# First mixer of a two-layer trunk: the value and gate block as one float32 product, and some copies and scalings on ScalarE

## The chip, the core and the metric
The kernel runs on one core of a Trainium2 chip. The metric is the device time of one execution in microseconds (us); lower is better. The engines are TensorE (PE; its weight loads PEld), VectorE (DVE), ScalarE (ACT), GpSimd (POOL) and SyncE (SP), which issues the transfers. Each engine takes its own instructions in order and waits on semaphores of the others.

## The reference, cut to what matters
Input x is 256 tokens of 1024 numbers. Two layers follow, each a mixer and a mixture of experts with layer norms. The change lies in the first layer's mixer:

```python
proj = x @ w_in
qa, kc, vc, ksl, vsl, kw, vw, ga, qm, km, vm = jnp.split(proj, EVEN_SPLITS, axis=-1)
qa = rope(heads(qa, NSA_HEADS), positions)       # kc, ksl, kw likewise
gates = jax.nn.sigmoid(ga.astype(jnp.float32)).astype(x.dtype).reshape(B, S, NSA_HEADS, 3)
o_a = nsa_attention(qa, kc, heads(vc, NSA_KV_HEADS), ksl, heads(vsl, NSA_KV_HEADS),
                    kw, heads(vw, NSA_KV_HEADS), gates, ...)
o_b = moba_attention(rope(heads(qm, MOBA_HEADS), positions),
                     rope(heads(km, MOBA_HEADS), positions), heads(vm, MOBA_HEADS))
return jnp.concatenate([o_a, o_b], axis=-1) @ w_out
```
Inside nsa_attention, keys and values (kc, vc) are compressed: overlapping blocks of 32 tokens, a position term, a two-layer network with gelu, and softmax scores of the queries against the 15 compressed blocks. With 256 tokens the selected-block branch and the window branch both reduce to causal softmax attention over all tokens.

## The kernel before, in words
Tokens lie in two tiles of 128 (t = 0, 1; NT = 2), the 1024 inputs in eight chunks of 128 (NCH = 8). The projection runs in six blocks of columns: w0[0] (kc, ksl, kw, vc; 512 columns), w0g (vsl, vw, gates; 280), w0[1] (queries of A; 512), then w0[2] to w0[4] (queries, keys, values of B). "First", "second" and "third block" below are the first three of these.

For accuracy a block is split: ACT rounds the weights to fp32r (wh, L190, in `split`), DVE subtracts to get the remainder (wl, L193), x has been split likewise (xh, xl), and `proj_nat` adds three products per chunk and token tile on PE (L244 xh·wh, L245 xl·wh, L246 xh·wl): 48 products a block. wh and wl of two chunks share a buffer of three. The accumulators `acc` are four banks. The unsplit x lies in xr, in one of six buffers (wp) that the weight blocks also use, so the transfer of a later block waits until xr is free. `proj_whole` is the form without splits, eight float32 products per token tile; before the change it is used only in layer 1's projection, for one token tile at a time (L254).

Around the second block, in the order of the code: the angles and the tables COS and SIN (`rope_tables`: DVE L148 to L162, sincos on ACT L164, then a table load on ACT, L169/L170 on DVE), the rotation of the first block's keys (`rope`, DVE L300 to L303, into rk) and the copy of vc (vcn, ACT L685), the second block, its copies (kv L692, gates L693 on DVE, their exponential L694 on ACT), and the router's constants: PE L178 sums wr against lnT, ACT copies the row to rrow (L180), PE spreads it with L182. Then come the third block and its rotation and transposes, then the compression: dup (each head's 64 columns twice side by side, DVE L717), transposes on PE (L718), two copies on ACT into Dt (L719, L720), the position term on DVE (XC, L724), w1 on PE (L732), gelu as a chain on DVE with its exponential on ACT (ge, L743 to L750), a transpose (L752), w2, scores against the compressed keys (L780), their softmax on DVE and ACT (cs, cm, pc; L786 to L803) and the transposes of pc (L309 in `transp4`).

The attention itself goes in pairs of heads (`nsa_pair`, `moba_pair`): scores on PE, `softmax` (largest value on DVE L579; exponential with its sum on ACT L581, one for each of the two heads; reciprocal, gate, and the scaling of P on DVE L586, one for each head), transposes of P (L595), products with the values.

The scheduler behind the code decides in which order each engine gets its instructions, by its own planning of times; it moves projection products of later blocks between the steps of the compression and of the softmax. So an edit in one line moves instructions elsewhere.

## Time and profile before
| | |
|---|---|
| median of 3 runs | 533.94 us (533.82 to 534.5) |
| profiled execution, own time | 533.85 us |
| its span | 531.9 us |
| PE / DVE / ACT busy, share of the span | 94% / 54% / 42% |
| mean granted TensorE clock | 0.989 |

The span runs from the first to the last instruction that the profile shows; the rest of the time lies around it. Busy time is the time in which an engine has an instruction under way. The first mixer takes the time to about 150 us, then come its output's layer norm and the router, layer 0's experts, and the second layer. In the timelines, a wait stands in brackets at the instruction that waited, with the instruction that released it.

### The profile page before, as it was taken

To read this page: it belongs to the slowest core of one execution; us is meant where nothing else is said; L and a number is where in the kernel's file an instruction comes from. 1 tells how busy PE (TensorE), PEld (TensorE's weight loads), DVE (VectorE), ACT (ScalarE), POOL (GpSimd) and SP (SyncE) were. 2 spreads that over 40 slices of the span, in tenths; PEclk is the share of its full clock that TensorE was granted. 3 is DMA by queue.
4 is the path that set the end of the run, shared out by engine and by line. 5 is a ranking of instruction groups with operands and counts; after the bars stand their busy time and mean duration, and the time that the engine had idled before them with its cause. 6 is when DMAs were issued, how large, how long until landed. Compare 5 with 4: busy or idle time off the path is not lost.

```text
span 531.9 us, 8516 instructions
## 1 busy us (share of the span) xinstructions
PE 501.4 (94%) x3201; PEld 316.4 (59%) x3201; DVE 289.5 (54%) x824; ACT 220.8 (42%) x433; POOL 7.6 (1%) x18
## 2 busy tenths in 40 slices
PE   8899989999999999999899999999999999999980
PEld 6687656676676354543354996898777454363320
DVE  5878796849669621221166555555648861141125
ACT  4545645547556121121144347556747321131022
POOL 1000000000020000000000000000002000000000
PEclk9999999999999999999999999999999999999995
DMA  8999500009938999999997980003976599999952
GB/s 243 381 429 429 217 0 1 1 0 393 412 152 322 415 363 335 421 422 422 432 430 307 370 341 1 0 1 147 427 297 238 224 394 342 402 423 419 427 217 84
DMA packets 25536, 150.02 MB, mean 282 GB/s; under 512 B 3472, under 2 KB 4112, under 8 KB 14992
## 3 DMA queue, kind: packets, MB, share of 16 engines
q1 hardware_dynamic: 25488, 149.41, 70.1%
q8 instruction: 27, 0.44, 0.3%
q14 instruction: 21, 0.17, 0.1%
HBM read 148.35 MB, written 1.05 MB: 281 GB/s over the span
## 4 chain that ended last, share of the span: by engine, by line
PE 82%; DVE 9%; ACT 4%; DMA 2%; issue 1%; SPq 0%; ACTq 0%; DVEq 0%
PE pmt L1264 16%; PE pmt L1296 9%; PE pmt L1231 4%; PE acc L1305 3%; PE acc L246 3%; PE acc L245 3%; PE acc L398 3%; PE acc L244 3%; PE acc L396 3%; PE acc L397 3%; PE acc L254 3%; DMA wb<-w 2%; PE acc L268 2%; PE acc L266 2%; PE acc L267 2%; PE z L880 2%
## 5 line engine op out<-in xcount | busy, mean ns | idle before, releaser
L1264 PE MATMUL pmt<-wgu,xg 128*64 128x512 f32 (+1 forms) x512 | 92.8, 595 | 0.0
L1264 PEld LDWEIGHTS pmt<-wgu,xg 128*64 128x64 f32 (+1 forms) x512 | 27.2, 123 | 52.9 <-issue 50.8
L190 ACT ACTIVATE wh<-wb 128x1024 fp32r<-128x1024 f32 (+2 forms) x44 | 41.1, 944 | 37.4 <-PE acc L267 19.7
L193 DVE TENSOR_TENSOR wl<-wb,wh 128x512 fp32r<-128x512 f32 (+1 forms) x72 | 45.1, 660 | 19.0 <-ACT wh L190 18.9
L1296 PE MATMUL pmt<-wd,hT 128*64 128x512 f32 (+1 forms) x256 | 53.9, 597 | 0.9 <-ACT hT L1280 0.9
L198 DVE TENSOR_TENSOR yl<-pmt,yh 128x512 fp32r<-128x512 f32 x20 | 13.8, 690 | 47.5 <-ACT yh L190 47.5
L246 PE MATMUL acc<-wl,xhl 128*128 128x512 f32 (+1 forms) x96 | 37.7, 395 | 1.5 <-DVE wl L193 1.5
L244 PE MATMUL acc<-wh,xhl 128*128 128x512 f32 (+1 forms) x96 | 37.3, 389 | 1.4 <-ACT wh L190 1.4
L245 PE MATMUL acc<-wh,xhl 128*128 128x512 f32 (+1 forms) x96 | 37.0, 386 | 0.0
L1272 DVE SCALAR_TENSOR_TENSOR hh<-pmt,cs,silu 128x256 f32<-128x256 f32 x12 | 5.8, 484 | 56.8 <-ACT silu L1270 56.8
L1270 ACT ACTIVATE silu<-pmt 128x256 f32<-128x256 f32 x12 | 4.6, 384 | 76.1 <-PE pmt L1264 76.1
L190 ACT ACTIVATE yh<-pmt 128x512 fp32r<-128x512 f32 x20 | 11.9, 597 | 55.9 <-PE pmt L1296 55.9
L1296 PEld LDWEIGHTS pmt<-wd,hT 128*64 128x64 f32 (+1 forms) x256 | 15.3, 123 | 27.0 <-issue 24.9
L1231 PEld LDWEIGHTS pmt<-Poh,xhl 128*128 128x128 f32 x192 | 24.4, 188 | 5.3 <-issue 3.2
L266 PE MATMUL acc<-xhl,wh 128*128 128x256 f32 x96 | 27.5, 287 | 0.0
L1231 PE MATMUL pmt<-Poh,xhl 128*128 128x256 f32 (+1 forms) x192 | 26.7, 292 | 0.3 <-DVE xg L1239 0.3
L268 PE MATMUL acc<-xhl,wl 128*128 128x256 f32 x96 | 26.9, 280 | 0.0
L267 PE MATMUL acc<-xhl,wh 128*128 128x256 f32 x96 | 26.8, 279 | 0.0
L398 PE MATMUL acc<-xol,oT 128*128 128x512 f32 x64 | 26.1, 412 | 0.0
L396 PE MATMUL acc<-xo,oT 128*128 128x512 f32 x64 | 25.9, 410 | 0.0
L397 PE MATMUL acc<-xo,oT 128*128 128x512 f32 x64 | 25.5, 401 | 0.0
L581 ACT ACTIVATE Pm<-pst,nm 128x128 f32<-128x128 f32 (+1 forms) x48 | 19.8, 419 | 10.7 <-DVE nm L579 9.5
(368 smaller groups left out, 984.0 us busy)
## 6 DMA issues: line engine op xcount, KB each, us to landing
wd<-wd SPq DMA_DIRECT2D x34, 1024.0 KB, 11.0
wgu<-wgu SPq DMA_DIRECT2D x64, 512.0 KB, 11.1
wgu<-wgu SPq DMA_DIRECT2D x14, 2048.0 KB, 12.1
wb<-w1s SPq DMA_DIRECT2D x6, 2048.0 KB, 19.1
wo<-wo SPq DMA_DIRECT2D x4, 2048.0 KB, 16.2
wgu<-wgu SPq DMA_DIRECT2D x8, 1024.0 KB, 7.2
wb<-w SPq DMA_DIRECT2D x3, 2048.0 KB, 22.0
wb<-w SPq DMA_DIRECT2D x2, 1024.0 KB, 8.9
```

Of the source, the lines that this page charges most:

```text
L190: A.activation(dst_h, src, AF.Copy)
L193: V.tensor_tensor(dst_l[:, i], src[:, i], dst_h[:, i].bitcast(F32), OP.subtract)
L244: PE.matmul(a[t][:, :n], xh[:, cc, ts], wh[:, c, :n], start=(cc == 0), stop=False)
L245: PE.matmul(a[t][:, :n], xl[:, cc, ts], wh[:, c, :n], start=False, stop=False)
L246: PE.matmul(a[t][:, :n], xh[:, cc, ts], wl[:, c, :n], start=False, stop=(cc == NCH - 1))
L266: PE.matmul(o, wh[:, c, fs], xh[:, cc], start=(cc == 0 and f % 2 == 0), stop=False, skip_group_check=True)
L396: PE.matmul(a[t][h], oc[:, 0, ts], wh[:, hs], start=first, stop=False)
L397: PE.matmul(a[t][h], oc[:, 1, ts], wh[:, hs], start=False, stop=False)
L398: PE.matmul(a[t][h], oc[:, 0, ts], wl[:, hs], start=False, stop=last)
L1231: PE.matmul(p[:, 0:w], src[:, t, c * 128:c * 128 + 128], P[:, t, u * 128:u * 128 + w], start=(t == 0 and src is xh), stop=(t == 1 and src ...
L1264: PE.matmul(pg[r, :], g[:, c, BASE[u] + r.start:BASE[u] + r.stop], ws[k, c], start=(c == 0), stop=(c == NCH - 1), tile_position=(0, r.start))
L1296: PE.matmul(y[r, :], hT[:, fc, r], wd[k][:, fc, h * 512:h * 512 + 512], start=(fc == 0), stop=(fc == 1), tile_position=(0, r.start))
```

## The change
Three edits, and one adapted call. The second block is done by `proj_whole` on the unsplit xr, for both token tiles, chunk by chunk: 16 float32 products of 128x280 (L255 in the changed kernel) in place of 48, without its 4 ACT and 8 DVE splits. In `softmax` the second head's P is scaled by ACT instead of DVE (24 of the 48 scalings of a run). The eight dup copies are done by ACT instead of DVE. Line numbers after the edits are up by one to three.

```diff
-    def proj_whole(a, wv, xT, t):
+    def proj_whole(a, wv, xT, ts=range(NT)):
         for c in range(NCH):
-            PE.matmul(a, xT[:, c, t * 128:t * 128 + 128], wv[:, c], start=(c == 0), stop=(c == NCH - 1))
+            for t in ts:
+                PE.matmul(a[t], xT[:, c, t * 128:t * 128 + 128], wv[:, c], start=(c == 0), stop=(c == NCH - 1))
...
-            for b in range(2):
-                V.tensor_scalar(P[:, b, 0:W], P[:, b, 0:W], ssum[:, b:b + 1], None, op0=OP.mult)
+            V.tensor_scalar(P[:, 0, 0:W], P[:, 0, 0:W], ssum[:, 0:1], None, op0=OP.mult)
+            A.activation(P[:, 1, 0:W], P[:, 1, 0:W], AF.Copy, scale=ssum[:, 1:2])
...
-        a = proj_nat(pp, wv1, 280, xh, xl)
+        a = [acc()[:, 0:280] for _ in range(NT)]
+        proj_whole(a, wv1, xr)
...
-                    V.tensor_copy(dup.rearrange("p (r d) -> p r d", r=2), s64.unsqueeze(1).to_broadcast([128, 2, 64]))
+                    A.activation(dup.rearrange("p (r d) -> p r d", r=2), s64.unsqueeze(1).to_broadcast([128, 2, 64]), AF.Copy)
...
-                proj_whole(va[i - 1], wbox[0], box[0], i - 1)
+                proj_whole(va, wbox[0], box[0], [i - 1])
```

**The end of the second block.** PE, from the block's last products to the third block's first. Before:
```order
L245 MATMUL acc<-wh,xhl 128x280
L246 MATMUL acc<-wl,xhl 128x280
L178 MATMUL pmt<-wr,lnT 2x20 x16
L244 MATMUL acc<-wh,xhl 128x512
L245 MATMUL acc<-wh,xhl 128x512
L182 MATMUL pmt<-rrow,identf 128x20 x4
L246 MATMUL acc<-wl,xhl 128x512
```
After:
```order
L255 MATMUL acc<-wb,xr 128x280 x16
L178 MATMUL pmt<-wr,lnT 2x20 x14
L182 MATMUL pmt<-rrow,identf 128x20 x2
L178 MATMUL pmt<-wr,lnT 2x20 x2
L244 MATMUL acc<-wh,xhl 128x512
L245 MATMUL acc<-wh,xhl 128x512
L182 MATMUL pmt<-rrow,identf 128x20 x2
L246 MATMUL acc<-wl,xhl 128x512
```
The first half of the router's L182, which reads rrow, moved ahead of the third block's first products; before, all of it came behind two of them.

ACT at the same place, from the tables to the router's second copy. Before:
```order
L190 ACTIVATE wh<-wb 128x2x280
L164 ACTIVATE sincos<-ang 128x128
L80 ACT_TABLE_LOAD
L190 ACTIVATE wh<-wb 128x2x280 x2
L685 ACTIVATE vcn<-acc 128x128
L190 ACTIVATE wh<-wb 128x2x280
L685 ACTIVATE vcn<-acc 128x128
L190 ACTIVATE wh<-wb 128x1024 x3
L180 ACTIVATE rrow<-pmt 2x20 x2
L694 ACTIVATE gat<-gat 128x48
```
After:
```order
L164 ACTIVATE sincos<-ang 128x128
L80 ACT_TABLE_LOAD
L190 ACTIVATE wh<-wb 128x1024 x3
L686 ACTIVATE vcn<-acc 128x128
L719 ACTIVATE dup<-rk 128x128
L686 ACTIVATE vcn<-acc 128x128
L719 ACTIVATE dup<-rk 128x128
L180 ACTIVATE rrow<-pmt 2x20
L696 ACTIVATE gat<-gat 128x48
L180 ACTIVATE rrow<-pmt 2x20
```
Three splits of the third block moved ahead of vcn; dup copies of rk stand ahead of both rrow copies, and the gates' exponential between these.

DVE there, from the tables through the rotation of the first block (`rk`, `ropetmp`) to the splits or copies behind it. Before:
```order
L193 TENSOR_TENSOR wl<-wb,wh 128x280 x2
L300 TENSOR_TENSOR rk<-acc,COS 128x384
L301 TENSOR_TENSOR ropetmp<-acc,SIN 128x6x32
L302 TENSOR_TENSOR ropetmp<-acc,SIN 128x6x32
L300 TENSOR_TENSOR rk<-acc,COS 128x384
L303 TENSOR_TENSOR rk<-rk,ropetmp 128x384
L301 TENSOR_TENSOR ropetmp<-acc,SIN 128x6x32
L302 TENSOR_TENSOR ropetmp<-acc,SIN 128x6x32
L193 TENSOR_TENSOR wl<-wb,wh 128x280
L303 TENSOR_TENSOR rk<-rk,ropetmp 128x384
L193 TENSOR_TENSOR wl<-wb,wh 128x280 x3
L193 TENSOR_TENSOR wl<-wb,wh 128x512 x2
```
After:
```order
L193 TENSOR_TENSOR wl<-wb,wh 128x512 x4
L301 TENSOR_TENSOR rk<-acc,COS 128x384
L302 TENSOR_TENSOR ropetmp<-acc,SIN 128x6x32
L303 TENSOR_TENSOR ropetmp<-acc,SIN 128x6x32
L301 TENSOR_TENSOR rk<-acc,COS 128x384
L304 TENSOR_TENSOR rk<-rk,ropetmp 128x384
L302 TENSOR_TENSOR ropetmp<-acc,SIN 128x6x32
L303 TENSOR_TENSOR ropetmp<-acc,SIN 128x6x32
L193 TENSOR_TENSOR wl<-wb,wh 128x512
L304 TENSOR_TENSOR rk<-rk,ropetmp 128x384
L193 TENSOR_TENSOR wl<-wb,wh 128x512
L694 COPY kv<-acc 128x256
```
Four splits of 512 columns stand ahead of the rotation where two of 280 stood; behind it there is one, where there were five.

**The compression.** ACT, at the last Dt copies. Before:
```order
L719 ACTIVATE Dt<-pmt 64x256
L720 ACTIVATE Dt<-pmt 64x255
L581 ACTIVATE Pm,ssum<-pst,nm 128x128 x2
L190 ACTIVATE wh<-wb 128x1024
L581 ACTIVATE Pm,ssum<-pst,nm 128x128 x2
L738 ACTIVATE hid<-pmt 30x128 x2
```
After:
```order
L719 ACTIVATE dup<-rk 128x128
L719 ACTIVATE dup<-vcn 128x128
L582 ACTIVATE Pm,ssum<-pst,nm 128x128
L721 ACTIVATE Dt<-pmt 64x256
L722 ACTIVATE Dt<-pmt 64x255
L719 ACTIVATE dup<-vcn 128x128 x2
L582 ACTIVATE Pm,ssum<-pst,nm 128x128
L721 ACTIVATE Dt<-pmt 64x256
L722 ACTIVATE Dt<-pmt 64x255
L719 ACTIVATE dup<-vcn 128x128
L582 ACTIVATE Pm,ssum<-pst,nm 128x128
L587 ACTIVATE Pm<-Pm,ssum 128x128
```
Dup copies and exponentials of the first pair's softmax moved between the Dt copies; ahead of the rows shown stand one more dup copy and the first two Dt copies, behind them the last two; before, all eight Dt copies follow each other. (The other two dup copies stand at the place shown above.)

ACT a little later, from the two copies of hid to the exponential of ge. Before:
```order
L738 ACTIVATE hid<-pmt 30x128 x2
L581 ACTIVATE Pm,ssum<-pst,nm 128x256
L747 ACTIVATE ge<-ge 64x128
L581 ACTIVATE Pm,ssum<-pst,nm 128x256
L190 ACTIVATE wh<-wb 128x1024
```
After:
```order
L740 ACTIVATE hid<-pmt 30x128 x2
L582 ACTIVATE Pm,ssum<-pst,nm 128x256 x2
L190 ACTIVATE wh<-wb 128x1024
L749 ACTIVATE ge<-ge 64x128
L587 ACTIVATE Pm<-Pm,ssum 128x256
```
A split of a later block and one more exponential moved ahead of the exponential of ge.

DVE, from the masked exponentials of the compressed scores (`cs`, tile number in the name) to pc. Before:
```order
L795 TENSOR_TENSOR cs_694<-cs_694,cmok 128x120 x2
L303 TENSOR_TENSOR rq<-rq,ropetmp 128x512
L796 TENSOR_REDUCE cm_699<-cs_694 128x16
L300 TENSOR_TENSOR rq<-acc,COS 128x512
L797 TENSOR_SCALAR cm_699<-cm_699 128x16
L301 TENSOR_TENSOR ropetmp<-acc,SIN 128x8x32
L798 RECIPROCAL cm_699<-cm_699 128x16
L302 TENSOR_TENSOR ropetmp<-acc,SIN 128x8x32
L800 TENSOR_TENSOR cm_699<-cm_699,gat 128x8 x2
L303 TENSOR_TENSOR rq<-rq,ropetmp 128x512
L803 TENSOR_TENSOR pc<-cs_694,cm_699 128x4x15 x4
```
After:
```order
L797 TENSOR_TENSOR cs_642<-cs_642,cmok 128x120 x2
L193 TENSOR_TENSOR wl<-wb,wh 128x512
L798 TENSOR_REDUCE cm_647<-cs_642 128x16
L193 TENSOR_TENSOR wl<-wb,wh 128x512
L799 TENSOR_SCALAR cm_647<-cm_647 128x16
L193 TENSOR_TENSOR wl<-wb,wh 128x512
L800 RECIPROCAL cm_647<-cm_647 128x16
L193 TENSOR_TENSOR wl<-wb,wh 128x512
L802 TENSOR_TENSOR cm_647<-cm_647,gat 128x8 x2
L193 TENSOR_TENSOR wl<-wb,wh 128x512
L805 TENSOR_TENSOR pc<-cs_642,cm_647 128x4x15 x4
```
Splits of a later block stand between the steps where the rotation of queries (`rq`) stood. On PE, 127 projection products of 128x512 stand ahead of the transposes of pc after, 112 before; ahead of the first product with the values, 135 and 117.

## Rows read from the trace of the kernel before

**Rows 1.** The table by stretches of the core's time: start and end in us, length, then busy time of each engine (with its count of instructions), granted clock, share of the DMA engines, GB/s. The stretches are the second block, the end of the compression, and the softmax part.
```profile
19.67:31.23 11.56, 8.67 (x82) 7.37 (x80) 10.02 (x36) 6.80 (x10) 0.00 (x0) 1.00 0.91 377
62.50:75.00 12.50, 10.51 (x62) 8.01 (x63) 10.22 (x40) 6.25 (x19) 0.00 (x0) 1.00 0.00 1
75.00:150.00 75.00, 74.72 (x432) 50.25 (x432) 53.20 (x154) 40.39 (x116) 0.00 (x0) 1.00 0.40 162
```

**Rows 2.** Timeline of PE over the second block and the start of the third: start us, us from start to end, engine, line, operation, out<-in and tile, count, and in brackets the idle time before it with what ended it. Ends of matmuls are modelled; the distance of two starts is the time that one takes.
```profile
19.91 0.29 PE L244 MATMUL acc<-wh,xhl 128*128 128x280 f32 x1
...
23.48 0.40 PE L244 MATMUL acc<-wh,xhl 128*128 128x280 f32 x1 [1.35 <-ACT wh L190]
...
27.14 0.39 PE L246 MATMUL acc<-wl,xhl 128*128 128x280 f32 x1 [1.36 <-DVE wl L193]
...
30.00 0.29 PE L245 MATMUL acc<-wh,xhl 128*128 128x280 f32 x1
30.13 0.29 PE L246 MATMUL acc<-wl,xhl 128*128 128x280 f32 x1
30.35 0.96 PE L178 MATMUL pmt<-wr,lnT 128*2 128x20 f32 x32
31.23 0.50 PE L244 MATMUL acc<-wh,xhl 128*128 128x512 f32 x1
31.57 0.40 PE L245 MATMUL acc<-wh,xhl 128*128 128x512 f32 x1
31.90 1.06 PE L182 MATMUL pmt<-rrow,identf 2*128 2x20 f32 x8
32.89 0.50 PE L246 MATMUL acc<-wl,xhl 128*128 128x512 f32 x1
```

**Rows 3.** Timeline of PE in layer 1's projection ahead of its mixer, where the program has float32 products of 128x512 without splits: sixteen in a row.
```profile
277.28 7.13 PE L254 MATMUL acc<-wb,xT 128*128 128x512 f32 x16 [0.15 <-ACT xT L316]
```

**Rows 4.** Timeline of ACT over the second block.
```profile
21.13 0.31 ACT L164 ACTIVATE sincos<-ang 128x128 f32<-128x128 f32 x1 [2.68 <-DVE ang L162]
21.46 1.28 ACT L80 ACT_TABLE_LOAD   x1
...
26.76 0.28 ACT L685 ACTIVATE vcn<-acc 128x128 f32<-128x128 f32 x1 [0.56 <-DVE ropetmp L302]
...
28.83 1.06 ACT L190 ACTIVATE wh<-wb 128x1024 fp32r<-128x1024 f32 x1 [0.85 <-PE acc L245]
...
31.34 0.23 ACT L180 ACTIVATE rrow<-pmt 2x20 f32<-2x20 f32 x2
31.47 0.23 ACT L694 ACTIVATE gat<-gat 128x48 f32<-128x48 f32 x1
```

**Rows 5.** Timeline of DVE over the second block.
```profile
19.14 0.94 DVE L159 SCALAR_TENSOR_TENSOR ang<-kk,ang 128x128 f32<-128x128 f32 x3
20.00 0.44 DVE L193 TENSOR_TENSOR wl<-wb,wh 128x280 fp32r<-128x280 f32 x1
20.36 0.19 DVE L160 TENSOR_SCALAR ang<-ang 128x64 f32<-128x64 f32 x1
20.46 0.44 DVE L193 TENSOR_TENSOR wl<-wb,wh 128x280 fp32r<-128x280 f32 x1
20.82 0.22 DVE L162 TENSOR_SCALAR ang<-ang 128x128 f32<-128x128 f32 x1
...
24.18 0.55 DVE L300 TENSOR_TENSOR rk<-acc,COS 128x384 f32<-128x384 f32 x1
...
27.00 0.55 DVE L303 TENSOR_TENSOR rk<-rk,ropetmp 128x384 f32<-128x384 f32 x1
...
29.75 0.42 DVE L692 COPY kv<-acc 128x256 f32<-128x256 f32 x1
...
31.11 0.17 DVE L693 TENSOR_SCALAR gat<-acc 128x24 f32<-128x24 f32 x1
```

**Rows 6.** Timeline of PE in the compression.
```profile
62.91 0.24 PE L752 MATMUL pmt<-identf,hid 64*128 64x64 f32 x1 [0.84 <-DVE ssum L584]
...
68.18 0.40 PE L245 MATMUL acc<-wh,xhl 128*128 128x512 f32 x1
68.41 0.40 PE L246 MATMUL acc<-wl,xhl 128*128 128x512 f32 x1
...
73.22 0.68 PE L309 MATMUL pmt<-identf,pc 128*128 128x128 f32 x4 [1.38 <-DVE pc L803]
```

**Rows 7.** Timeline of ACT in the compression.
```profile
52.51 0.38 ACT L719 ACTIVATE Dt<-pmt 64x256 f32<-64x256 f32 x1 [0.86 <-DVE XC L724]
...
60.42 0.30 ACT L747 ACTIVATE ge<-ge 64x128 f32<-64x128 f32 x1
...
61.08 1.05 ACT L190 ACTIVATE wh<-wb 128x1024 fp32r<-128x1024 f32 x1
```

**Rows 8.** Timeline of DVE in the compression.
```profile
59.23 0.69 DVE L579 TENSOR_REDUCE nm<-pst 128x2 f32<-128x512 f32 x1
...
73.38 1.29 DVE L193 TENSOR_TENSOR wl<-wb,wh 128x512 fp32r<-128x512 f32 x2
```

**Rows 9.** The softmax's exponentials (ACT) and scalings (DVE) over the whole run: engine, operation, count, ns least/median/most of one, first and last start, forms.
```profile
L581 ACT ACTIVATE Pm<-pst,nm x48: 348/424/487, 54.1 to 141.9; 128x128 f32<-128x128 f32 x24, 128x256 f32<-128x256 f32 x24
L586 DVE TENSOR_SCALAR Pm<-Pm,ssum x48: 276/316/353, 55.8 to 143.4; 128x128 f32<-128x128 f32 x24, 128x256 f32<-128x256 f32 x24
```


## The prediction, made before the run

> **What bounds the kernel now.** I read four views in this order: the table by stretches, then the timelines of PE, ACT and DVE over the two places that the change touches. The table [rows 1] says where the change can act at all. In the second block's stretch PE is busy 8.67 of 11.56 us, in the stretch that ends with the compression 10.51 of 12.50, and from 75 to 150 us, where the softmax work lies, it is busy 74.72 of 75.00. So PE sets the time of the softmax part, and there a lighter DVE or a heavier ACT is worth nothing until PE has to wait for it. Only in the first two stretches is PE short of work.
>
> In the second block [rows 2] PE's products stand 0.13 us apart (30.00 to 30.13), but the block lasts from 19.91 to 30.35: PE waits 1.35 us for an ACT split at 23.48 and 1.36 for a DVE split at 27.14. Behind the ACT split stand sincos and the 1.28 us table load [rows 4]. PE then does the router's constants (L178, L182) around the third block's first products and runs without gaps from 32.89. In the compression [rows 6] it waits 0.84 us before the transpose at 62.91 and 1.38 before the one at 73.22.
>
> **The change part by part.**
>
> *Work removed and added on PE.* 48 products at 0.13 are 6.2 us [rows 2]. The 16 new ones are float32 with 280 columns, a shape that this trace lacks. The nearest row is the float32 product with 512 columns: 16 in 7.13 us, 0.45 each [rows 3]. Bounds are therefore 0.13 (the split form with the same columns) and 0.45 (the same form with more columns), 2.1 and 7.1 us for 16. I take the float32 row scaled by columns, 0.45 × 280/512 = 0.245, so 3.9 us. PE's work falls by 2.3 us. Started at 19.91, the block ends at 23.8 and L178, of which 7/8 now stands ahead of the first L182 (0.84 of 0.96 us), at 24.65; at the upper bound, at 27.9.
>
> A rule speaks against this term. The 512-column row is 0.45 us against 0.23 for the split form of the same width [rows 3, 6], a factor of two. The Trainium skill, "FP8 and Floating Point Precision", section "TensorE Precision Notes", says that true float32 takes four passes through the array. By that page, as an estimate, 16 products would cost 4 × 0.13 × 16 = 8.3 us and PE's work would grow by 2.1 us instead; the block would end at 28.2 and L178 at 29.05. The trace does not agree, and goes before it. Even so the end of the next paragraph's wait would stay where it is, only its cover would shrink from 5.0 to 0.6 us.
>
> *The wait that replaces the stalls.* In the changed order PE's next instruction after L178 is L182, which reads rrow, and rrow stands on ACT behind three splits of the third block, both vcn copies and two dup copies; the second dup reads rk of the second token tile, which DVE's last rope addition writes. In the order before, rrow stood ahead of nothing that PE needed early. So I follow that chain.
> - DVE: L159 ends at about 20.0, and the two splits of 0.36 net that stood among the last three angle steps (20.00 to 20.36, 20.46 to 20.82) are gone [rows 5]. sincos moves from 21.13 to 20.41, the table load ends at 22.02 [rows 4].
> - ACT: three splits of 1.05 [rows 4] from 22.03 end at 23.1, 24.1 and 25.15.
> - DVE: four splits of the third block, 0.65 each (1.29 for two [rows 8]), now stand ahead of the rope: 23.1 to 24.4, then, bound by the second ACT split, to 25.5. Rope starts at 25.5 instead of 24.18. Before, it took 24.18 to 27.55 with one 280-column split inside [rows 5]; that one is now 512 wide, about 0.25 longer, so 3.6 us: rk is done at 29.1.
> - ACT: the dup copy. Nearest rows are the 128x128 copy, 0.28, and a 128x128 exponential, 0.35 at least [rows 4, 9]; I take 0.3. rrow follows, 0.23: 29.65. L182 starts there, five microseconds after PE came to it.
> - The second half: four L178, L244 and L245 (0.67 us together from 31.23 to 31.90, as L182 follows L245 [rows 2]) run to 30.6. The second rrow stands behind the gates' exponential, which needs both kv copies and both gat steps on DVE. These took 29.75 to 31.11 with a 512-wide split among them [rows 5]; without it about 0.85. After rk (29.1) and one split (0.6) they run from 29.7 to 30.55; exponential and rrow to 30.95; L182, now half of the 0.99 us between 31.90 and 32.89, ends at 31.5.
>
> So the dense part begins at 31.5 instead of 32.89: **1.4 us** earlier, not the 5 that work and stalls together would give. Ends: if rope overlaps the splits better than I count, 2.4; if dup and rrow each wait for one more split, 0.3. The weights now stay in plain float32 until 23.8, so the buffer of xr is freed later and a transfer of the fourth or fifth block can start later; its data are read some 20 us on, and I cost that at nothing.
>
> *Dup copies in the compression.* Here ACT was the link before: eight Dt copies, then exponentials. In the changed order five dup copies (0.28), three exponentials (about 0.36 each) and a scaling (0.36) stand between the first Dt copy and the last: 1.4 + 1.1 + 0.36 = 2.85 us, of which the 0.86 that ACT waited there [rows 7] takes some. XC and the w1 products come 2.0 us later. In the gelu chain a 1.05 us split now stands ahead of the exponential of ge, which ran before it (60.42, then 61.08 [rows 7]): I count 0.8, since DVE's 0.69 reduction [rows 8] no longer stands inside the chain. Between the sum over cs and pc stand five 512-wide splits, 3.2 us, in place of rope steps of about 2: 1.2. Together pc's transposes come **4.0 us later** on their chain. But PE does 15 projection products more ahead of them (127 instead of 112, by the order), 0.23 each (68.18 to 68.41 [rows 6]): 3.5 us of work brought forward. Up to the first value products it is 18, 4.2 us. Net loss 0.5 at the first point, about 0 at the second; I take **0.3**. Ends: a gain of 2.2 (both waits of rows 6 gone, since DVE is lighter) and a loss of 4.0 (none of the products were missing later).
>
> *Second head's scaling.* 24 DVE steps of 0.28 to 0.35 become 24 ACT steps; the exponentials of the same shapes, 0.35 to 0.49, bound them from above [rows 9]. Both heads are now scaled side by side instead of in turn, which saves about 0.3 a softmax, and an ACT split of 1.05 can stand in front, which costs up to that. PE covers either with projection and output products [rows 1]. I take 0, with ends of -0.3 and +2.
>
> The call in the second layer's projection does the same products in the same order: 0.
>
> **Sum.** On the profiled execution: 533.85 - 1.4 + 0.3 = 532.75. The span is 531.9, so 1.95 us lie around it and stay. The median of the runs is 0.09 higher: 532.84, **532.8 us**. After 150 us nothing in the change touches the order of layer 0's expert products in a way that I can price; their weight loads wait for the router, so the shift should pass through.
>
> **The rivals.**
> - *More: the lighter DVE also closes the compression's waits.* For it: DVE is busy 10.22 of 12.50 us there [rows 1]. Against it: five splits and ACT's copies stand in the chain. Price: 0.84 + 1.38 = 2.2 gone instead of 0.3 lost; 533.94 - 1.4 - 2.2 = 530.3.
> - *Slower: the products brought forward are missing later.* They fill the waits of the compression, but they were the cover of the softmax chains from 75 to 150 us, where PE had 0.28 us of idle time [rows 1]. If the 4.2 us of cover is missed by half, the time is 532.8 + 2.1 = 534.9, if wholly, 537.0. For it: the scaling on ACT lengthens the same chains when a split is ahead. Against it: output products become available as each pair ends. It decides if PE's waits after 75 us exceed 2.2 us.
> - *Nothing: the third block starts no earlier.* If rk is done 1 us later than I count, or the second rrow waits for one more DVE split, the 1.4 shrinks to 0.3, which the compression takes: 533.9.
>
> **How the numbers follow.** About 0.2%, 1.07 us, is what a measurement of this kernel can tell from no change; the forecast lies at that edge (532.87). Forecast 0.50 (531.9 to 533.7; 0.28 faster, 0.22 same), more gain 0.14 (faster), slower 0.22 (0.19 slower, 0.03 same), nothing 0.14 (0.12 same, 0.02 slower). So faster 0.42, same 0.37, slower 0.21. The range runs from the rival of more gain, 530.3, to somewhat past the middle price of the slower one, 535.5, and leaves about 0.15 out.
>
> **What would show it.** In the changed profile: 16 float32 products from about 19.9 to 23.8; then PE idle for some 5 us until L182, released by rrow of ACT at about 29.65; dense products from 31.5; the pc transposes about 2.6 us later than 73.22 (4.0 less 1.4) with PE's wait there still over 1 us; from 75 to 150 us less than 0.7 us of idle. It is wrong if L182 does not wait, if PE waits for Pm or for splits after 75 us, or if the float32 products take over 0.4 us each.

## The result and the profile after

The changed kernel takes **538.37 us** (median of 20 runs, 535.24 to 543.09), the kernel before 534.08 beside it (20 runs, 532.69 to 536.46). The ratio is 1.0077, with an interval of 1.006 to 1.0094: **slower by 0.8%**, some 4.1 us. The forecast was 532.8 us, and the range ended at 535.5. The profiled execution of the changed kernel took 539.2 us, its span is 537.4. Further down, medians count every run and ratios only the fast ones: one run each of e4, e9 and e10 was slow (1243.57, 828.11 and 715.89 us).

Changed kernel, table by stretches (start, end, length, busy time of each engine with its instructions, granted clock, DMA share, GB/s). The first is the second block up to the third, the second holds the end of the compression, and the last two are the softmax part and what comes behind it:
```profile
21.92:31.36 9.44, 9.44 (x71) 7.47 (x69) 7.91 (x20) 4.36 (x9) 0.00 (x0) 1.00 0.86 356
65.50:78.00 12.50, 11.10 (x66) 8.66 (x62) 10.51 (x36) 4.86 (x14) 0.00 (x0) 1.00 0.00 1
75.00:150.00 75.00, 73.92 (x432) 48.86 (x431) 48.36 (x135) 48.68 (x138) 0.00 (x0) 1.00 0.44 169
150.00:165.00 15.00, 11.73 (x100) 8.99 (x100) 10.71 (x38) 8.79 (x18) 2.96 (x4) 1.00 0.52 195
```
The kernel before, the last of these stretches, which no row ahead of the prediction shows:
```profile
150.00:165.00 15.00, 14.46 (x132) 11.58 (x131) 11.91 (x51) 11.57 (x22) 2.79 (x4) 1.00 0.48 190
```
Against [rows 1]: the second block's stretch has no hole left, the softmax part has 1.08 us of idle PE instead of 0.28, and between 150 and 165 us PE is idle for 3.27 us instead of 0.54. The holes have moved from the start of the mixer to behind its end.

Changed kernel, timeline of PE at the start, over the second block, at the transposes of pc, and from the last value products (PT,vm) into the router:
```profile
5.05 2.08 PE L229 MATMUL acc<-wh,xhl 128*128 128x512 f32 x4 [0.60 <-ACT wh L190]
...
22.16 7.71 PE L255 MATMUL acc<-wb,xr 128*128 128x280 f32 x32
...
30.62 0.62 PE L182 MATMUL pmt<-rrow,identf 2*128 2x20 f32 x4
...
32.57 0.50 PE L246 MATMUL acc<-wl,xhl 128*128 128x512 f32 x1
...
77.28 0.60 PE L310 MATMUL pmt<-identf,pc 128*128 128x128 f32 x4
...
148.95 0.87 PE L672 MATMUL pmt<-PT,vm 128*64 128x256 f32 x8
...
152.60 1.08 PE L310 MATMUL pmt<-identf,xn 128*128 128x128 f32 x8
...
160.17 2.02 PE L328 MATMUL pmt<-oneb 128*128 128x256 bf16 x17
164.91 0.66 PE L328 MATMUL pmt<-rge,oneb 128*128 128x160 bf16 x7 [2.72 <-DVE rge L979]
```
The kernel before, the same engine, where the earlier rows show nothing:
```profile
4.85 1.21 PE L229 MATMUL acc<-wh,xhl 128*128 128x512 f32 x4 [0.40 <-ACT wh L190]
...
145.24 0.87 PE L671 MATMUL pmt<-PT,vm 128*64 128x256 f32 x8
...
151.16 1.03 PE L309 MATMUL pmt<-identf,xn 128*128 128x128 f32 x8
...
158.69 2.02 PE L327 MATMUL pmt<-oneb 128*128 128x256 bf16 x17
160.76 0.65 PE L327 MATMUL pmt<-rge,oneb 128*128 128x160 bf16 x7
```
Three things can be read from these. First, the 16 float32 products of the second block are **32 records** and last 7.7 us, not 3.9. Second, against [rows 6] the transposes of pc come at 77.28 instead of 73.22, and the last values at 148.95 instead of 145.24. Third, the router's first rank product (rge, oneb: for each token the comparisons that order its experts) waits 2.72 us for DVE; before, it waited for nothing, as the 17 keep-warm products ahead of it (oneb alone, dummies whose result nobody reads) ran right up to it. Its distance from the last values is 15.96 us, against 15.52.

In this execution the first products also ran slowly (four in 2.08 us instead of 1.21), so that the second block began 2.26 us late. Of the experiments below, two profiles show the same (e11 1.87 and e3 1.49 us late), the others lie within 0.45 us of the kernel before; the edits don't touch that place.

What DVE, GpSimd and ACT do ahead of the rank product, changed kernel:
```profile
162.24 0.73 DVE L975 TENSOR_TENSOR rge<-lg 128x160 bf16<-128x160 f32 x1
162.90 0.84 DVE L976 TENSOR_TENSOR rgt<-lg 128x160 bf16<-128x160 f32 x1
163.66 0.76 DVE L977 TENSOR_TENSOR rge<-rge,before 128x160 bf16<-128x160 bf16 x1
```
```profile
161.36 2.96 POOL L509 TENSOR_TENSOR xhl<-xn,xhl 128x256 fp32r<-128x256 f32 x4 [158.73 <-ACT lnst L358]
```
```profile
158.96 1.23 ACT L485 ACTIVATE xn<-xn,lnst 128x1024 f32<-128x1024 f32 x1
160.10 0.19 ACT L357 ACTIVATE lnst<-lnst 128x1 f32<-128x1 f32 x1
160.22 1.06 ACT L506 ACTIVATE xhl<-xn 128x1024 fp32r<-128x1024 f32 x1
161.18 0.19 ACT L358 ACTIVATE lnst<-lnst 128x1 f32<-128x1 f32 x1
```
The same steps of the kernel before, DVE, GpSimd and then the first tile's norm and split on ACT:
```profile
159.56 0.32 DVE L973 TENSOR_TENSOR rge<-lg 128x160 bf16<-128x160 f32 x1
159.79 0.32 DVE L974 TENSOR_TENSOR rgt<-lg 128x160 bf16<-128x160 f32 x1
160.03 0.23 DVE L975 TENSOR_TENSOR rge<-rge,before 128x160 bf16<-128x160 bf16 x1
```
```profile
156.05 2.79 POOL L508 TENSOR_TENSOR xhl<-xn,xhl 128x256 fp32r<-128x256 f32 x4 [153.42 <-DVE lnst L346]
```
```profile
153.63 1.24 ACT L484 ACTIVATE xn<-xn,lnst 128x1024 f32<-128x1024 f32 x1 [0.81 <-DVE lnst L483]
154.91 1.06 ACT L505 ACTIVATE xhl<-xn 128x1024 fp32r<-128x1024 f32 x1
```
Before, GpSimd had finished the lower half of the first token tile's split (the subtraction into xhl) at 158.84, ahead of DVE's rank steps. Now it runs from 161.36 to 164.32, over them, and three steps take 0.73, 0.84 and 0.76 instead of 0.32, 0.32 and 0.23: 1.46 us. On ACT the first tile's norm and split (1.23 and 1.06) now start at 158.96 and 160.22 instead of 153.63 and 154.91, before and between the two small steps (L357, L358) that the second tile's rank waits for.

### The profile page after: what moved, and what is told of

It reads as the page before. It is cut to its first block, busy times and chain, and to the rows that moved or that the text cites. A ratio compares the mean times of both kernels' runs of the same rounds, so it can differ in the third digit from the quotient of the medians.

```text
span 537.4 us, 8469 instructions
## 1 busy us (share of the span) xinstructions
PE 507.1 (94%) x3185; PEld 318.0 (59%) x3185; DVE 282.3 (53%) x784; ACT 228.7 (43%) x461; POOL 7.7 (1%) x18
## 4 chain that ended last, share of the span: by engine, by line
PE 85%; DVE 7%; ACT 5%; issue 1%; DMA 1%; SPq 0%; DVEq 0%
PE pmt L1266 16%; PE pmt L1298 9%; PE pmt L1233 4%; PE acc L255 4%; PE acc L1307 3%; PE acc L246 3%; PE acc L244 3%; PE acc L245 3%; PE acc L397 3%; PE acc L399 3%; PE acc L398 3%; PE acc L229 2%; PE acc L267 2%; PE acc L269 2%; PE acc L268 2%; PE pst L619 2%
## 5 line engine op out<-in xcount | busy, mean ns | idle before, releaser
L1266 PE MATMUL pmt<-wgu,xg 128*64 128x512 f32 (+1 forms) x512 | 95.2, 607 | 0.0
L1298 PE MATMUL pmt<-wd,hT 128*64 128x512 f32 (+1 forms) x256 | 55.8, 611 | 0.9 <-ACT hT L1282 0.9
L190 ACT ACTIVATE wh<-wb 128x1024 fp32r<-128x1024 f32 (+1 forms) x40 | 38.4, 971 | 39.0 <-PE acc L268 19.9
L193 DVE TENSOR_TENSOR wl<-wb,wh 128x512 fp32r<-128x512 f32 x64 | 41.7, 684 | 22.3 <-ACT wh L190 22.2
L246 PE MATMUL acc<-wl,xhl 128*128 128x512 f32 x80 | 32.8, 410 | 1.4 <-DVE wl L193 1.4
L244 PE MATMUL acc<-wh,xhl 128*128 128x512 f32 x80 | 32.7, 408 | 0.0
L245 PE MATMUL acc<-wh,xhl 128*128 128x512 f32 x80 | 32.4, 405 | 0.0
```

The lines of the kernel that those rows point to most:

```text
L190: A.activation(dst_h, src, AF.Copy)
L193: V.tensor_tensor(dst_l[:, i], src[:, i], dst_h[:, i].bitcast(F32), OP.subtract)
L244: PE.matmul(a[t][:, :n], xh[:, cc, ts], wh[:, c, :n], start=(cc == 0), stop=False)
L245: PE.matmul(a[t][:, :n], xl[:, cc, ts], wh[:, c, :n], start=False, stop=False)
L246: PE.matmul(a[t][:, :n], xh[:, cc, ts], wl[:, c, :n], start=False, stop=(cc == NCH - 1))
L1266: PE.matmul(pg[r, :], g[:, c, BASE[u] + r.start:BASE[u] + r.stop], ws[k, c], start=(c == 0), stop=(c == NCH - 1), tile_position=(0, r.start))
```

## The experiments

Each time is a median beside runs of the kernel before in the same set (534.24 to 534.68 us), with the ratio and its interval; the ratio compares the two sets as a whole and is not the quotient of the medians. To compare profiles, this is how much later than in the kernel before PE starts the same instruction (us). "Start" is the second block's first product, "rrow" the last L182, "pc" the transposes of pc, "values" the first of the last eight PT,vm, "rank" the first rge,oneb; the last column is the distance from values to rank. (The expectations of e5, e6 and e10 count from the last of the eight, some 0.6 us later: 15.4 us in the changed kernel, 13.6 in e6.)

| kernel | start | rrow | pc | values | rank | values to rank |
|---|---|---|---|---|---|---|
| before (at) | 19.91 | 32.70 | 73.22 | 145.24 | 160.76 | 15.52 |
| changed | +2.26 | -0.33 | +4.06 | +3.71 | +4.15 | 15.96 |
| float32 alone | -0.15 | -0.98 | +2.12 | +2.07 | +2.07 | 15.53 |
| scaling alone | 0 | -0.54 | +0.16 | +0.74 | +1.18 | 15.97 |
| dup alone | +1.49 | -0.35 | +4.43 | +1.03 | +1.93 | 16.43 |
| changed, e5 | +0.04 | -1.35 | +3.06 | +2.69 | +3.09 | 15.92 |
| changed, e6 | +0.32 | -1.66 | +2.71 | +2.33 | +1.01 | 14.20 |
| float32, constants later still, e12 | +0.14 | moved | -4.98 | -3.22 | -3.23 | 15.53 |

**e1, e2, e3: one part each.** The theory was that the parts on ACT (scaling, dup) cost the time, and the rival that the float32 block does. The float32 products alone:
```diff
-        a = proj_nat(pp, wv1, 280, xh, xl)
+        a = [acc()[:, 0:280] for _ in range(NT)]
+        proj_whole(a, wv1, xr)
```


> Only the second block in float32; dup copies and both scalings stay on DVE. Theory (the loss comes from the router's tail and the compression, which the scalings and the dup copies reorder; the block itself ends inside the wait for rrow): PE reaches L182 at about 28.5 us, waits about 1 us for rrow, and the third block is dense from about 31.5 instead of 32.89; the tail keeps the order of before; 0.5 to 1.5 us faster than before. Rival (PE bounds, so the 1.5 us of additional PE work count in full): 1.5 us slower than before.

Measured 535.52, ratio 0.9999 (0.9972 to 1.0025): neither the theory's gain nor the rival's loss. Its own table by stretches:
```profile
28.00:32.00 4.00, 2.35 (x26) 1.67 (x21) 4.00 (x15) 0.83 (x5) 0.00 (x0) 0.97 1.01 434
32.00:36.00 4.00, 4.00 (x12) 3.19 (x12) 0.33 (x2) 0.29 (x2) 0.00 (x0) 0.60 1.01 430
...
64.00:68.00 4.00, 4.00 (x26) 3.45 (x24) 1.22 (x6) 2.87 (x9) 0.00 (x0) 0.74 0.02 4
68.00:72.00 4.00, 4.00 (x15) 2.84 (x15) 3.22 (x14) 0.40 (x1) 0.00 (x0) 0.50 0.01 2
```
The third block starts 1 us earlier, and then the granted clock falls: 0.60 over 32 to 36 us, where 12 products run in 4 us, and 0.50 (the 1.2 GHz level) over 68 to 72 us. Ahead of the first fall PE had waited for rrow and was busy 2.35 of 4 us. From rrow to pc, over the two falls, this execution gives back 3.1 us.

The scaling alone (e2), and the dup copies alone (e3):
```diff
-            for b in range(2):
-                V.tensor_scalar(P[:, b, 0:W], P[:, b, 0:W], ssum[:, b:b + 1], None, op0=OP.mult)
+            V.tensor_scalar(P[:, 0, 0:W], P[:, 0, 0:W], ssum[:, 0:1], None, op0=OP.mult)
+            A.activation(P[:, 1, 0:W], P[:, 1, 0:W], AF.Copy, scale=ssum[:, 1:2])
```


> Only the second head's scaling on ACT. Theory: ACT gets the square root of the second token tile (its Ln and Exp) behind norm and split of the first tile in the router's tail, and the GpSimd subtraction falls on the DVE steps of the rank; 2 to 4 us slower than before, nearly all of it between the first transposes of xn and the rank's first product. Rival (the slow PE clock in the first 10 us of the profiled run made the change look slow): as before within 0.5 us, tail or no tail.


```diff
-                    V.tensor_copy(dup.rearrange("p (r d) -> p r d", r=2), s64.unsqueeze(1).to_broadcast([128, 2, 64]))
+                    A.activation(dup.rearrange("p (r d) -> p r d", r=2), s64.unsqueeze(1).to_broadcast([128, 2, 64]), AF.Copy)
```


> Only the dup copies on ACT. Theory: the compression's chain comes some 2 to 4 us later, PE fills it with 25 projection products that it brings forward (137 instead of 112 ahead of the transposes of pc), and some of these are missing later: 0 to 2 us slower than before; the tail keeps its order or nearly so. Rival (slow clock at the start): as before within 0.5 us.

Measured 538.86, ratio 1.0068 (1.0039 to 1.0097), and 537.25, ratio 1.0041 (1.002 to 1.0061). Either alone costs about half a per cent or more, and they don't add up: together with the block it is 0.77%. The table says why. The dup copies delay pc by 4.8 us from rrow, the scaling by 0.7, but both end in the same tail: between the last values and the transposes of xn (the first tile's norm, transposed for the router) stand 12 output products in e2 and 13 in e3, as in the changed kernel with its 12, where the kernel before has 22, and PE then waits 2.7 to 2.8 us for rge. In both the clock falls behind that wait, and the way from the rank product to the first gather product (Poh) takes 1.0 and 1.1 us longer than before. For e2 this goes beyond the one profile: the mean granted clock of its executions is 0.980, against 0.986 beside it; over 536 us that is 3.2 us of PE's work, as an estimate, of some 3.6 us that e2 loses. Timeline of PE in e3, and then the table by stretches of e2, with most of the wait in the first stretch:
```profile
162.69 1.12 PE L327 MATMUL pmt<-rge,oneb 128*128 128x160 bf16 x7 [2.83 <-DVE rge L977]
```
```profile
157.00:161.00 4.00, 2.21 (x21) 1.76 (x19) 2.80 (x9) 2.92 (x6) 2.61 (x4) 1.00 0.95 399
161.00:166.00 5.00, 4.06 (x31) 3.51 (x32) 4.49 (x20) 2.27 (x3) 0.35 (x1) 0.66 0.82 339
```

**e4, e5, e6, e7: the tail.** Two causes were on the table: the order on ACT and DVE (the first tile's work ahead of the second's small steps), and the collision of GpSimd with DVE's rank steps. e4 puts the first tile's ACT split behind the second tile's exponential, e5 issues the second tile's sum behind the first tile's chain, as it stood in time before; both are the changed kernel otherwise, and the edits hold for layer 0 alone.
```diff
-            A.activation(xhl[:, 0, 0], x[:, 0], AF.Copy)
+            with (tc.issue_after(last["A"]) if l == 0 else nullcontext()):
+                A.activation(xhl[:, 0, 0], x[:, 0], AF.Copy)
```


> The changed kernel, with the ACT split of the first token tile in the router's tail put behind the second tile's Ln and Exp; nothing else differs. Theory: the second tile's Exp comes about 1.1 us earlier (160.1 instead of 161.2) and with it the rank's first product; the GpSimd subtraction starts where it did and now meets the later part of the DVE rank steps; 0.7 to 1.5 us faster than the changed kernel. Rival (the tail is not on the path, weight loads of layer 0 set its end): no difference to the changed kernel beyond 0.3 us.


```diff
-        sts[1] = ln_sum(x[:, 1], a[1])
+        with (tc.issue_after(last["m"]) if l == 0 else nullcontext()):
+            sts[1] = ln_sum(x[:, 1], a[1])
```


> The changed kernel; in the router's tail of layer 0 DVE finishes the sum of token tile 0 before it begins that of tile 1. The split and the GpSimd subtraction stay as they are. Theory (the tail's loss is the order of ACT and DVE there, about 1.4 us, and the overlap of the GpSimd subtraction with the rank steps on DVE, about 1.5): tile 0's chain comes 0.6 us earlier, the subtraction starts about a microsecond earlier against the rank steps and meets fewer of them: the first rank product 0.5 to 1.5 us earlier after the last product with the values than the 15.4 us of the changed kernel. Rival (about 15 us from the last products with the values to the rank are fixed latency): 15.0 to 15.5 us.

Measured 538.46, ratio 1.0065 (1.0037 to 1.0094), and 539.05, ratio 1.0075 (1.0051 to 1.0099): either piece of the order alone gives nothing, against both theories. DVE in e4:
```profile
161.28 0.85 DVE L976 TENSOR_TENSOR rge<-lg 128x160 bf16<-128x160 f32 x1
162.05 0.85 DVE L977 TENSOR_TENSOR rgt<-lg 128x160 bf16<-128x160 f32 x1
162.82 0.77 DVE L978 TENSOR_TENSOR rge<-rge,before 128x160 bf16<-128x160 bf16 x1
163.50 0.76 DVE L979 TENSOR_TENSOR rgt<-rgt,behind 128x160 bf16<-128x160 bf16 x1
```
The rank steps start 0.6 us closer to the last values, and now four of them stand beside GpSimd (161.22 to 164.16) instead of three. e6 takes both edits and takes GpSimd out of the way: the first tile's subtraction goes to DVE, behind the rank steps, with the same values.
```diff
-            for h in range(4):
+            for h in range(0 if l == 0 else 4):
...
+            for h in range(2 if l == 0 else 0):
+                hs = slice(h * 512, h * 512 + 512)
+                V.tensor_tensor(xl[:, 0, hs], x[:, 0, hs], xh[:, 0, hs].bitcast(F32), OP.subtract)
```


> The changed kernel with e5's order, the second tile's Ln and Exp ahead of the split, and tile 0's subtraction on DVE behind the rank steps instead of on GpSimd (the same values). Theory: the DVE rank steps take 0.2 to 0.35 us each instead of 0.73 to 0.85; 12.8 to 13.5 us from the last values to the rank's first product, and, less up to 1.3 us of DVE time behind it, 1 to 2.3 us faster than the changed kernel. Rival (fixed latency): 15 us again, no faster, or slower by the 1.3 us.

Measured 536.43, ratio 1.0028 (1.0007 to 1.0049): against the kernel before, 0.49% or some 2.6 us less than the changed kernel. Its DVE and PE:
```profile
160.58 0.32 DVE L977 TENSOR_TENSOR rge<-lg 128x160 bf16<-128x160 f32 x1
160.81 0.32 DVE L978 TENSOR_TENSOR rgt<-lg 128x160 bf16<-128x160 f32 x1
161.05 0.23 DVE L979 TENSOR_TENSOR rge<-rge,before 128x160 bf16<-128x160 bf16 x1
```
```profile
161.77 0.66 PE L328 MATMUL pmt<-rge,oneb 128*128 128x160 bf16 x7 [1.09 <-DVE rge L981]
...
165.77 1.40 PE L1238 MATMUL pmt<-Poh,xhl 128*128 128x256 f32 x9 [0.82 <-DVE xhl L1096]
```
The steps are back at 0.32 and 0.23, and from values to rank it takes 14.20 us instead of 15.96. Of these 1.76 us, 1.48 lie behind the start of the rank steps (1.19 us to the rank product instead of 2.67) and 0.28 ahead of it. The GpSimd part moved away by itself was not run. Some 0.8 us of it go where the subtraction now stands, ahead of the gather products. e7 is e6 without the float32 block and without the dup copies on ACT (the scaling and the tail alone).

> Only the second head's scaling on ACT, with the tail of e6. Theory: the 1.5 us by which the mixer's products end earlier in e2 now reach the experts: 1 to 2.5 us faster than before. Rival (the mixer's end hangs on the last products with the values, which came 0.7 us later in e2, and a fixed chain): 0.5 us slower than before or more.

Measured 535.04, ratio 1.0007 (0.9983 to 1.0031), against 1.0068 for the scaling without the tail's edits: with the tail mended, nothing that can be measured is left of its cost. The gain that its theory expected did not come.

**e8, e9, e12: what the float32 block is worth.** In e1 and in the changed kernel the router's constants hold the third block up, for rrow. These kernels have the float32 block alone, with the call that makes the constants moved behind the third block's transposes (e8), or behind the first pair of the mixer's softmax part (e9; e12 is e9 once more).
```diff
-        if not cur.get("consts"):
-            cur["consts"] = True
-            router_consts()
+        first = not cur.get("consts")
+        cur["consts"] = True
...
+        if first:
+            router_consts()
```


> Only the second block in float32 (as e1), and the router's constants (L178, L182) moved behind the third block's transposes in the program. Theory (in e1 PE waits at L182 for rrow, and the clock falls after that idle time): the third block starts at about 27.6 us right behind the float32 products, the granted clock stays at 1.00 up to 60 us, and the median is 2 to 3 us below before. Rival (the third block cannot start before the rotation has freed its banks or its splits are there, about 30 us): 0 to 1 us below before.

> Only the second block in float32, with the router's constants moved behind the first pair of the softmax part in the program (e8 had them ahead of the compression, where its clock fell). Theory (what ends the mixer is the chain rotation, compression, pairs, last products with the values, and about 15 us behind these; the third block started 4.7 us earlier in e8 and the router's constants and the clock took that back ahead of the compression): the transposes of pc come 3 to 4.7 us earlier than in the kernel before, the last products with the values 2 to 3, and the median is 1.5 to 3 us below before. Rival (PE's work bounds the softmax part, and the float32 block has 1.5 us more of it): the last products with the values come at most 1 us earlier, whatever the compression gains; 0 to 1 us below before.

> The kernel of e9 once more, on a chip of its own with other runs of before beside it. Theory (its gain is real, and its profile lost 1.5 us to a fall of the clock at 60 to 68 us that need not come in each execution): ratio 0.994 to 0.999, last products with the values 1.7 to 3.5 us earlier than in the kernel before, 3.3 without a fall of the clock. Rival (e9's gain was the scatter of the runs): ratio 1.000 or above.

Measured 534.62 (0.9991, 0.9968 to 1.0015), 532.8 (0.9971, 0.9943 to 0.9999) and 531.49 (0.9961, 0.9935 to 0.9987). In all three the third block's dense part starts some 4.8 us sooner (its first L246 at 28.0 to 28.3 instead of 32.89). e8 loses most of it again where the constants now stand (its last values come 0.8 us early), and its theory, full clock up to 60 us and a gain of 2 to 3 us, missed. Its table by stretches:
```profile
46.00:48.00 2.00, 2.00 (x14) 1.55 (x15) 1.04 (x4) 0.46 (x3) 0.00 (x0) 0.85 1.05 451
48.00:50.00 2.00, 2.00 (x9) 1.50 (x7) 1.07 (x5) 0.97 (x3) 0.00 (x0) 0.50 1.00 418
```
They take about 1.9 us from 44.78 on, and behind these tiny products the clock falls to the 1.2 GHz level. e9 and e12 are one program; the stretches of e9, then those of e12:
```profile
56.00:60.00 4.00, 3.19 (x19) 1.99 (x17) 3.67 (x12) 2.95 (x11) 0.00 (x0) 1.00 0.72 303
60.00:64.00 4.00, 4.00 (x22) 3.42 (x21) 0.91 (x6) 1.85 (x5) 0.00 (x0) 0.56 0.06 18
64.00:68.00 4.00, 4.00 (x14) 3.08 (x13) 4.00 (x15) 0.41 (x1) 0.00 (x0) 0.58 0.01 2
```
```profile
56.00:60.00 4.00, 3.19 (x18) 1.97 (x17) 3.68 (x12) 2.96 (x11) 0.00 (x0) 1.00 0.79 336
60.00:64.00 4.00, 4.00 (x30) 3.40 (x30) 2.02 (x10) 1.98 (x6) 0.00 (x0) 1.00 0.21 82
64.00:68.00 4.00, 2.86 (x13) 1.97 (x11) 4.00 (x15) 1.37 (x2) 0.00 (x0) 1.00 0.00 0
```
One execution lost some 1.5 us to the clock and kept 1.8 at the last values, the other lost none and kept 3.2, through to its end (530.56 in that execution). e12's other executions split the same way: seven with a mean granted clock of 0.988 or more have a median of 530.65, five below 0.986 one of 534.67. So the float32 block alone, with nothing of PE's waiting behind ACT at that place, makes a kernel that **beats both**, by 0.3 to 0.4% against the kernel before: 531.49 against 534.24.

**e10: the scaling on top of that.** e9 with the scaling on ACT and the tail of e6.

> e9 with the second head's scaling on ACT and the tail of e6; of the change only the dup copies stay on DVE. Theory: the compression is as in e9, the tail as in e6 (13.5 us from the last values to the rank, then about 0.9 us lost behind the DVE subtractions): within 1 us of e9. Rival (the scaling on ACT delays the pairs as such): the last products with the values over 1.5 us later than in e9, and the time as much above it.

Measured 534.33, ratio 1.0003 (0.9983 to 1.0023), 1.5 us above e9; the theory missed and the rival held. The last values come 1.85 us later than in e9 while the tail is 14.20: the scaling delays the pairs themselves. From pc to the last values, where neither profile has a fall of the clock, it takes 75.01 us instead of 73.70.

**e11: dummy work under the wait.** The changed kernel with 42 keep-warm products in layer 0's router instead of 17, 25 dummies that compute nothing.
```diff
-                keep_warm(17, pool)
+                keep_warm(42 if l == 0 else 17, pool)
```


> The changed kernel with 25 more of the dummy products that keep PE busy ahead of the rank in layer 0's router (42 instead of 17, some 2.7 us, about the wait that PE has there). They compute nothing that is used. Theory (the idle time there lets the clock fall in some executions, as in e2 to e4 where 161 to 171 us ran at 0.66 to 0.87): granted clock 1.00 from 160 to 175 us, the rank's first product where the changed kernel has it, and a median 0 to 1 us below the changed kernel's. Rival (the clock falls there for another reason, or not more often than elsewhere): no difference, or slower by what the dummy products delay the rank.

Measured 537.24, ratio 1.0057 (1.0032 to 1.0082). Its profile has no fall of the clock in the tail, the mean granted clock of its executions is 0.989, against 0.984 in the changed kernel, and the rank product comes as late after the last values as without it (15.97 us). So the dummies do hold the clock up. The intervals of the two kernels overlap, and whether the time follows is not settled.

## Why the prediction was wrong

**Failed: the compression's credit** ("PE does 15 projection products more ahead of them ... 3.5 us of work brought forward ... Net loss 0.5 at the first point, about 0 at the second; I take **0.3**"). The chain itself was sized well: pc comes 4.4 us later, counted from rrow, in the changed kernel and in e5 alike (predicted 4.0), and e3 shows that it is the dup copies (4.8 alone). What is wrong is the credit of 3.7 against it. In e5, whose start is undisturbed, the last values come 2.69 us late, where the prediction's sum put them 1.1 early.

The softmax pairs end nearly as late as they began, and the traces' counts show where the credit went: from pc to the last values PE has 15 projection products fewer (65 instead of 80), as predicted, but 11 output products more (73 instead of 62). At 0.23 each that is 0.9 us less, against 0.8 us more of idle PE in the changed kernel. PE did wait for Pm there, a sign of being wrong that the prediction named: 1.0 us in two waits. Each part on ACT shifts the output products by itself (73 in e2, 71 in e3), the float32 block does not (62 in e1). And the credit is not void as such: in e3, with 25 projection products fewer there and 9 output products more, pc is 4.43 us late and the last values 1.03.

The output products done sooner are real: 23 instead of 34 are left behind the last values (to the end of the second tile), 11 at 0.23, 2.5 us. But the layer's end does not hang on them. It hangs on the chain that the last values start: norm, router, ranks. In the prediction's terms this is its rival "the products brought forward are missing later", with the waits beyond the stretch where it looked: PE's idle time from 75 to 165 us is 1.08 + 3.27 = 4.35 us, against 0.28 + 0.54, past its point of 2.2. Its price for the whole, 537.0, is 1.4 below the median.

**Failed: "After 150 us nothing in the change touches the order of layer 0's expert products in a way that I can price; their weight loads wait for the router, so the shift should pass through."** The tail ahead of these products was put at nothing. No line of the change stands there, but how many products are left behind the last values sets when DVE may take up the second tile, and that sets the order on three engines. With 22 products ahead of xn DVE finished the first tile's norm before the second's sums; with 12 it does both at once, the first tile's norm ends later on ACT, and its GpSimd part falls onto the rank steps. That GpSimd part is most of what must go: e4 and e5 mend one piece of the order each and gain nothing, e6 mends both, moves the GpSimd part, and gains 1.8 us from values to rank, 1.5 of them in and behind the rank steps, and 0.49% of the time. With its edits the distance is 1.3 us shorter than in the kernel before (14.20 instead of 15.52), a third of the credit; that the products done sooner pay this is likely, but the kernel before with the same edits was not run.

With both, e5's profile is accounted for: predicted at rank -1.1, found +3.1; 3.8 of the 4.2 us stand at the last values and 0.4 in the tail. In the medians 1.0 to 1.3 us more are lost than that profile has at the rank product (4.1 us for the changed kernel and 4.4 for e5, against 3.1). Falls of the clock and slow starts, which some profiles show and some don't, fit that and fit the wider spread (535 to 543): the two slowest executions (541.18 and 543.09) have the lowest mean granted clock, 0.976. Over the changed kernel's 20 executions the mean is 0.984, over the 111 of the kernel before that stand beside the experiments 0.987; over 536 us the difference is some 1.7 us of PE's work, an estimate from above, as a fall costs less where PE waits anyway. e11, at 0.989, keeps a ratio of 1.0057, so by that run some 3 us are no matter of the clock. In the changed profile itself 4.15 of the 5.5 us at the span's end stand at the rank product; from 495 to 505 us its clock is 0.83 where the kernel before has 1.00. What the slow starts cost in the medians was not measured.

**Right end, wrong cover: the second block.** The float32 product was priced at 0.245 us and takes 0.48. Sixteen records in [rows 3] were taken as sixteen products; they are eight, since a float32 product leaves two records, as x32 for 16 products shows after (7.71 us). Read so, the row gives 0.89 for 512 columns and 0.487 for 280, 7.8 us for the block. The estimate from the Trainium skill's four passes ("FP8 and Floating Point Precision", section "TensorE Precision Notes"), which the prediction set aside, was 8.3 us: with 7.7 the trace comes near it, and the sentence that it does not agree was wrong. PE's work in the block grew by 1.5 us (7.7 instead of 6.2) where the prediction had it fall by 2.3. The error did not reach the sum, for the reason that the prediction gave: the end of that stretch is set by rrow. Timeline of PE in e5:
```profile
29.60 0.62 PE L182 MATMUL pmt<-rrow,identf 2*128 2x20 f32 x4 [1.17 <-ACT rrow L180]
...
31.54 0.50 PE L246 MATMUL acc<-wl,xhl 128*128 128x512 f32 x1
```
L182 starts at 29.60 (predicted 29.65) and the dense part at 31.54 (31.5), with 1.2 us of waiting instead of 5. In the profile of the changed kernel the late start hides even that. The gain of 1.35 us is there, and e1 shows that by itself it is worth nothing that can be measured (0.9999). In its profiled execution the clock took it back; over its 12 executions the mean granted clock is hardly lower than beside it (0.985 and 0.986), so that the falls explain this for the median is not shown.

**Scaling, taken as 0, with an end of +2.** e10 against e9 makes it +1.5 us with the tail mended; e7 cannot tell it from nothing. As the changed tail stands it costs more, 0.68% or some 3.6 us alone. The bound of +2 was too low because it ended at the softmax, not at the router.

## What to carry to other kernels

Before work that is done sooner is credited to an engine, find what ends the stage last: if it is a chain, filler done earlier shortens the stage only where the chain's own steps come sooner by it. In e3 they did (3.4 of 4.4 us came back by the last values), in the changed kernel other filler took the place, and PE idled at the end instead. A change in the amount of filler also changes the order of the other engines behind it, so look at DVE, ACT and GpSimd where the stage ends, not only where the edit is. And check how many records one instruction leaves, against the order of the program, before dividing a row's time by its count.

## What the runs showed of the hardware

**GpSimd and DVE.** A DVE step of 0.23 to 0.32 us took 0.73 to 0.85 while GpSimd's subtraction of 128x256 ran beside it (2.96 us for four, 0.74 each), in all the profiles quoted above in which they meet, and 0.23 to 0.32 where GpSimd was moved away (e6): each step took about one GpSimd instruction. The Trainium skill ("SBUF — State Buffer", section "Who interferes with whom") says that a DVE instruction with two SBUF inputs contends with a GpSimd instruction that reads SBUF, and that the port pair the two share is an exclusive lock; these rows agree with it, as the slow steps read both inputs from SBUF.

**The clock.** The granted clock fell to the 1.2 GHz level, for a few microseconds, behind stretches in which PE had waited (busy 2.35 of 4 us in e1, 2.21 of 4 in e2, 3.19 of 4 in e9) or had run the router's tiny products (e8); e1 lost 3.1 us over two falls, e9 some 1.5, e2 1.0. The same program as e9 kept the full clock in e12 behind 3.19 of 4 us and behind 2.86 of 4, so these runs don't tell when it falls, only that one or two microseconds of waiting can cost as much again.

**The first products.** In three of the profiles (the changed kernel, e3, e11) the first four took 2.07 to 2.08 us instead of 1.21, in five others (e5 to e9) 1.46 to 1.95. The 1.00 that the table prints for the granted clock there is no reading: each trace's clock record begins only some microseconds into the span, at 4.56 us in the kernel before, 10.22 in the changed kernel, 8.66 in e3 and 9.46 in e11, with the full level, and a time without a record is printed as 1.00. In these three traces the products start some 0.43 us apart ahead of that time and 0.23 to 0.24 behind it, about twice as fast, so the ones ahead of it look like the 1.2 GHz level. Why the full clock came later in some executions is open.
